# Letting the V side of a cross-covariance attention kernel fall behind and close after the loop

## The chip, the cores and the metric

The kernel runs on one core of one Trainium2 chip. The metric is the device time of a launch in microseconds (us), as the median of several executions. The profiles are taken in single executions; their span, from the first to the last instruction, is 1.7 to 1.8 us shorter than the device time of the same execution (two executions of one experiment differ by 2.1 and 3.0 us). Each run is filed as fast or slow; here slow means over 1.5% above the fastest run of the same kernel.

In lines of the profile PE is TensorE (PEld its weight loads), DVE is VectorE, ACT is ScalarE, POOL is GpSimd, and SPq is the queue of SyncE, which issues the transfers. The strips cut the span into 40 slices: PEclk is the clock granted to TensorE and DMA the busy share of the transfer engines, both in tenths. In a timeline the name after the line number is the operation, then written tile `<-` read tiles; `vb`, `vps`, `vt`, `po` and `so` are a V unit after the cast, its transposes, their copy, its product and the evicted product.

## The reference

```python
batch, heads, seq, dim = 8, 12, 512, 64                       # Q, K, V: float32
Q_norm = Q / (norm(Q, axis=-2) + 1e-10); K_norm = K / (norm(K, axis=-2) + 1e-10)
attn = softmax(einsum('bhnd,bhne->bhde', Q_norm, K_norm))     # 64 x 64 for each head
out  = einsum('bhnd,bhde->bhne', V, attn)
```

There are 96 heads. The kernel takes four at a time, a "unit", so 24 units. For each unit Q, K, V and the output are one transfer of 512 KB each.

## The kernel before

The two sides of a unit use different data until the last product. The attention side casts Q and K to bf16, forms Gram matrices, norms, logits and exponentials, normalises the result and writes a second copy of it ("doubled"). The V side casts V, transposes it on TensorE, evicts the transposes (copies them out of PSUM, the memory in which this kernel places what TensorE writes), multiplies by the attention matrix and evicts the product in two halves.

```python
def cast_v(u, copy=nc.scalar.copy):
    w = vb[u] = vbp.tile([128, SV, TP, 2 * D], BF16, name="vb")          # 3 buffers
    copy(w.rearrange("p s t d -> p s (t d)"), vf[u])

def vtrans(u):
    ps = ps_v.tile([128, SV, TP, 128], BF16, name="vps")                 # 1 buffer in PSUM
    for g in range(SV):
        for t in range(TP):
            nc.tensor.transpose(ps[:, g, t, :], vb[u][:, g, t, :], identb)
    w = vt[u] = vtp.tile([128, SV, TP, 128], BF16, name="vt")            # 3 buffers
    nc.scalar.copy(w, ps)

def outs(u):
    ...                                          # 2 halves of 8 matmuls into PSUM (po, 2 buffers)
        nc.scalar.copy(s[:, g], po)              # one eviction for each half

for s in range(U):                               # one iteration carries pieces of several units
    on(load_qk, s + 3); on(load_v, s + 1); on(store, s - 6)
    on(cast_v, s - 1);  on(cast_q, s + 1)
    on(scale_k, s - 1); on(normalise, s - 2)
    on(grams, s);       on(norms, s);    on(cast_k, s + 1)
    on(doubled, s - 2); on(keep_kq, s)
    on(outs, s - 3)
    on(logits, s - 1);  on(scale_q, s - 1); on(exps, s - 1)
    on(vtrans, s - 1)
...                                              # the last attention steps and outs(21), outs(22), outs(23)
```

The schedule is manual: the program's order is the order of each engine's instructions. In the trace of the kernel before, TensorE, VectorE and ScalarE start theirs in that order throughout iteration 23 and the tail; on VectorE, for instance, the normalisation of unit 22 starts at 123.17 us, the V cast after it at 123.51 and the first step of the next normalisation at 124.11. All 96 transfers are issued from SyncE, in one order.

Of the kernel before, what the change touches and what calls it, by code (L numbers as in the profile page):

```python
# [24 lines left out]
def kernel(  # L25
# [7 lines left out]
    nc = tc.nc  # L33
    B, H, N, _ = Q.shape
    assert N == NV * R and Q.shape[3] == D
    U = B * H // HU
# [17 lines left out]
    ps_o = ctx.enter_context(tc.tile_pool(name="ps_o", bufs=2, space=bass.MemoryType.PSUM))  # L54

    LOAD_AHEAD = 3
    V_AHEAD = LOAD_AHEAD - 2
    STORE_LAG = 6

    qf, kf, vf, vb, qkb, nsq, rq, kqs, sl, ex, vt, so, kq = ({} for _ in range(13))  # L60

    def load_qk(u):
        qf[u] = qp.tile([128, R, D], F32, name="qf")
        kf[u] = qp.tile([128, R, D], F32, name="kf")
        nc.sync.dma_start(out=qf[u].rearrange("p t d -> p (t d)"), in_=Qf[u])  # L65
        nc.sync.dma_start(out=kf[u].rearrange("p t d -> p (t d)"), in_=Kf[u])  # L66

    def load_v(u):
        vf[u] = vp.tile([128, SV, TP * 2 * D], F32, name="vf")
        nc.sync.dma_start(out=vf[u], in_=Vf[u])  # L70

    def store(u):
        nc.sync.dma_start(out=Of[u], in_=so[u].rearrange("p s t d -> p s (t d)"))
# [8 lines left out]
    def cast_v(u, copy=nc.scalar.copy):  # L82
        w = vb[u] = vbp.tile([128, SV, TP, 2 * D], BF16, name="vb")
        copy(w.rearrange("p s t d -> p s (t d)"), vf[u])  # L84
# [25 lines left out]
    def scale_k(u):  # L110

        kk = kqs[u] = small.tile([128, HU, D], F32, name="kqs")
        nc.vector.tensor_tensor(  # L113
            out=kk[D:], in0=kq[u][D:], in1=rq[u][D:, :, None].to_broadcast([D, HU, D]), op=ALU.mult,
        )

    def logits(u):
        for h in range(HU):
            nc.tensor.transpose(lg[:, h, :], kqs[u][D:, h, :], ident[D:, D:])  # L119
# [9 lines left out]
    def normalise(u):  # L129
        s = small.tile([D, HU], F32, name="esum")  # L130
        nc.vector.reduce_sum(out=s, in_=ex[u], axis=AX.X)
        ri = small.tile([D, HU], F32, name="rinv")
        nc.vector.reciprocal(ri, s)
        a = abuf[u % len(abuf)]
        nc.vector.tensor_tensor(out=a[0:D, :, 0, :], in0=ex[u], in1=ri[:, :, None].to_broadcast([D, HU, D]), op=ALU.mult)  # L135

    def vtrans(u):

        ps = ps_v.tile([128, SV, TP, 128], BF16, name="vps")
# [3 lines that stand above are left out]
        w = vt[u] = vtp.tile([128, SV, TP, 128], BF16, name="vt")  # L143
        nc.scalar.copy(w, ps)  # L144

    def doubled(u):

        a = abuf[u % len(abuf)]
        nc.tensor.matmul(dup[D:], identb[0:D, 0:D], a[0:D, :, 0, :], tile_position=(0, D))  # L149
        nc.scalar.copy(a[D:, :, 1, :], dup[D:])  # L150

    def outs(u):
        s = so[u] = sop.tile([128, SV, TP, 2 * D], F32, name="so")
        a = abuf[u % len(abuf)]
        for g in range(SV):
            po = ps_o.tile([128, TP, 2 * D], F32, name="po")
            for t in range(TP):
                for x in range(2):
                    rows = slice(MV * x, MV * (x + 1))
                    nc.tensor.matmul(  # L160
                        po[rows, t, :], vt[u][:, g, t, rows],
                        a[:, 2 * g + x].rearrange("p a d -> p (a d)"), tile_position=(0, MV * x),
                    )
            nc.scalar.copy(s[:, g], po)  # L164

    gbuf = ps_g.tile([128, HU, 512], F32, name="gram")
    ltile = ps_l.tile([128, 2, HU, D], F32, name="lgdup")
# [3 lines left out]

    for u in range(LOAD_AHEAD):
        load_qk(u)
        if u - 2 >= 0:
            load_v(u - 2)

    ident = const.tile([128, 128], F32, name="ident")
    make_identity(nc, ident)
# [2 lines left out]
    mhalf = const.tile([128, HU], F32, name="mhalf")  # L181
    nc.gpsimd.memset(mhalf, -0.5)
    abuf = []
    for i in range(3):
        a = const.tile([128, HU, 2, D], BF16, name=f"ab{i}")
        nc.gpsimd.memset(a, 0.0)
        abuf.append(a)

    def on(f, u):
        if 0 <= u < U:  # L190
            f(u)

    on(cast_q, 0)
    on(cast_k, 0)
    for s in range(U):
        on(load_qk, s + LOAD_AHEAD)
        on(load_v, s + V_AHEAD)
        on(store, s - STORE_LAG)
        on(cast_v, s - 1)
        on(cast_q, s + 1)  # L200
        on(scale_k, s - 1)
        on(normalise, s - 2)
        on(grams, s)
        on(norms, s)
        on(cast_k, s + 1)
        on(doubled, s - 2)
        on(keep_kq, s)
        on(outs, s - 3)
        on(logits, s - 1)
        on(scale_q, s - 1)  # L210
        on(exps, s - 1)
        on(vtrans, s - 1)


    last = U - 1
    scale_k(last)
    logits(last)
    scale_q(last)
    exps(last)
    normalise(last - 1)  # L220
    doubled(last - 1)
    outs(last - 2)
    cast_v(last, nc.vector.tensor_copy)
    normalise(last)
    doubled(last)
    vtrans(last)
    outs(last - 1)
    outs(last)
    for u in range(U - STORE_LAG, U):
        store(u)  # L230


# [28 lines left out]
```

## Time and profile before

| | before |
|---|---|
| device time, median of 3 runs | 134.80 us (134.79 to 135.32) |
| span of the profiled run | 134.2 us |
| bytes moved | 50.34 MB in 96 transfers |
| busy share PE / DVE / ACT / POOL | 67 / 71 / 72 / 28 % |

No engine is busy three quarters of the time, and the strip of the DMA engines reads 9 nearly everywhere. The prediction shows those lines. The busy shares average over a long middle, where transfers set the pace (DMA is 79% of the chain of waits), and a tail of 14 us, where a chain of small dependent steps does. A transfer lands 10.1 to 10.3 us after its issue (medians), and one takes 1.28 us at 409 GB/s; by estimate from these two about eight are under way at once. The change is about the tail.

### The profile page before, as it was taken

How to read it: one execution, taken by the hardware profiler on the slowest of the kernel's cores; microseconds unless marked ns; L12 is line 12 of the kernel's file. 1: busy time of each engine (PE TensorE's matmuls, PEld its weight loads, DVE VectorE, ACT ScalarE, POOL GpSimd, SP SyncE). 2: the span in 40 equal slices, each digit the busy share in tenths (PEclk: the TensorE clock that was granted, in tenths of full speed). 3: DMA queues.
4: the chain of work that ended last, by engine and by line, in shares of the span. 5: the costliest groups of instructions: out<-in, count | busy, mean ns of one | idle time of the engine just before them, and what ended most of it. 6: DMA issues, size and time to landing. Idle time of an engine off the chain costs nothing.

```text
span 134.2 us, 5393 instructions
## 1 busy us (share of the span) xinstructions
PE 89.5 (67%) x2232; PEld 69.9 (52%) x2232; DVE 95.6 (71%) x361; ACT 96.5 (72%) x168; POOL 37.3 (28%) x35
## 2 busy tenths in 40 slices
PE   0137659786689997864866766776776399964930
PEld 0136538664468685643744644555555287652720
DVE  0447859999998698989669679679679397767300
ACT  3000857989999789896867966966965779797760
POOL 7004440543225325431230330330330303311000
PEclk9999999999955558999689689779779755798555
DMA  4999999999999999999999999999999999998454
GB/s 150 330 393 412 401 402 404 398 396 404 398 401 407 411 402 415 403 405 408 405 411 417 400 412 410 413 407 419 401 413 401 416 407 400 406 385 316 153 201 173
DMA packets 19992, 50.67 MB, mean 378 GB/s; under 512 B 1537, under 2 KB 1537, under 8 KB 19969
## 3 DMA queue, kind: packets, MB, share of 16 engines
q1 hardware_dynamic: 19968, 50.34, 96.4%
q8 instruction: 17, 0.28, 0.8%
q14 instruction: 7, 0.05, 0.1%
HBM read 37.75 MB, written 12.58 MB: 375 GB/s over the span
## 4 chain that ended last, share of the span: by engine, by line
DMA 79%; ACT 7%; SPq 3%; PE 3%; issue 2%; DVE 2%; DVEq 0%; ACTq 0%
DMA vf<-in_V_dram 71%; DMA qf<-in_Q_dram 8%; ACT vb L84 2%; ACT so L164 2%; SPq L66 2%; SPq L65 1%; PE lgdup L119 1%; PE po L160 1%; ACT ab L150 1%; PE vps L142 1%; ACT vt L144 1%; DVE sl L123 1%; PE lgdup L149 1%; SPq L70 0%; DVE kqs L113 0%
## 5 line engine op out<-in xcount | busy, mean ns | idle before, releaser
L108 POOL TENSOR_TENSOR rq<-nsq,mhalf 128x4 f32<-128x4 f32 x24 | 34.9, 1453 | 83.2 <-DVE nsq L103 83.2
L91 PE MATMUL gram<-qkb 32*128 32x128 bf16 x1536 | 36.9, 264 | 9.3 <-DVE qkb L80 8.7
L91 PEld LDWEIGHTS <-qkb 32*128 32x128 bf16 x1536 | 31.1, 118 | 13.3 <-DVE qkb L80 9.0
L84 ACT CAST vb<-vf 128x1024 bf16<-128x1024 f32 x23 | 24.1, 1047 | 17.4 <-DMA vf<-in_V_dram 17.4
L164 ACT COPY so<-po 128x512 f32<-128x512 f32 x48 | 25.8, 589 | 0.9 <-PE po L160 0.2
L160 PEld LDWEIGHTS <-vt 128*64 128x64 bf16 x384 | 15.0, 133 | 19.3 <-issue 18.8
L144 ACT COPY vt<-vps 128x1024 bf16<-128x1024 bf16 x24 | 24.0, 1000 | 1.2 <-PE vps L142 0.9
L103 DVE CUSTOM_DVE_ANT_0 scr<-gram,ident 128x128 f32<-128x128 f32 x96 | 22.0, 282 | 2.3 <-PE gram L91 2.0
L77 DVE CAST qkb<-qf 128x1024 bf16<-128x1024 f32 x24 | 16.5, 686 | 7.9 <-DMA qf<-in_Q_dram 7.6
L123 DVE TENSOR_TENSOR sl<-lgdup,rq 64x256 f32<-64x256 f32 x24 | 10.0, 416 | 15.2 <-PE lgdup L119 13.7
L142 PE MATMUL vps<-identb,vb 128*128 128x128 bf16 x192 | 19.2, 260 | 1.7 <-ACT vb L84 1.7
L160 PE MATMUL po<-ab,vt 128*64 128x128 bf16 x384 | 19.5, 259 | 0.6 <-ACT so L164 0.6
L119 PE MATMUL lgdup<-ident,kqs 64*64 64x64 f32 x96 | 11.4, 249 | 12.7 <-ACT ab L150 12.1
L149 PE MATMUL lgdup<-ab,identb 64*64 64x256 bf16 x24 | 8.0, 334 | 15.6 <-DVE ab L135 15.2
L80 DVE CAST qkb<-kf 128x1024 bf16<-128x1024 f32 x24 | 16.4, 685 | 0.5 <-DMA kf<-in_K_dram 0.5
L142 PEld LDWEIGHTS <-vb 128*128 128x128 bf16 x192 | 14.1, 116 | 4.6 <-ACT vb L84 1.9
L119 PEld LDWEIGHTS lgdup<-ident,kqs 64*64 64x64 f32 x96 | 7.0, 122 | 16.6 <-ACT ab L150 14.9
L96 ACT COPY kq<-gram 64x256 f32<-64x256 f32 x24 | 8.8, 367 | 9.1 <-DVE nsq L103 8.8
L150 ACT CAST ab<-lgdup 64x256 bf16<-64x256 f32 x24 | 8.8, 367 | 3.1 <-PE lgdup L149 2.7
L113 DVE TENSOR_TENSOR kqs<-kq,rq 64x256 f32<-64x256 f32 x24 | 10.1, 422 | 1.1
L127 ACT ACTIVATE ex<-sl 64x256 f32<-64x256 f32 x24 | 10.0, 418 | 1.0 <-DVE sl L123 1.0
L135 DVE TENSOR_TENSOR ab<-ex,rinv 64x256 bf16<-64x256 f32 x24 | 10.0, 417 | 0.8
(15 smaller groups left out, 28.9 us busy)
## 6 DMA issues: line engine op xcount, KB each, us to landing
qf<-in_Q_dram SPq DMA_DIRECT2D x24, 512.0 KB, 10.3
kf<-in_K_dram SPq DMA_DIRECT2D x24, 512.0 KB, 10.3
vf<-in_V_dram SPq DMA_DIRECT2D x24, 512.0 KB, 10.3
out_dram<-so SPq DMA_DIRECT2D x24, 512.0 KB, 10.1
```

Of the source, the lines that this page charges most:

```text
L77: nc.vector.tensor_copy(qkb[u][:, :, 0:D], qf[u])
L80: nc.vector.tensor_copy(qkb[u][:, :, D:], kf[u])
L84: copy(w.rearrange("p s t d -> p s (t d)"), vf[u])
L91: nc.tensor.matmul(gbuf[:, h, 0:2 * D], x, x, start=(t == 0), stop=(t == R - 1), tile_position=(NV * h, 0))
L103: nc.vector.tensor_tensor_reduce(out=scr, in0=gbuf[:, h, 0:2 * D], in1=ident, scale=1.0, scalar=1e-20, op0=ALU.mult, op1=ALU.add, accum_ou ...
L108: nc.gpsimd.tensor_tensor(out=r, in0=n2, in1=mhalf, op=ALU.pow)
L119: nc.tensor.transpose(lg[:, h, :], kqs[u][D:, h, :], ident[D:, D:])
L123: nc.vector.tensor_tensor(out=s, in0=lg, in1=rq[u][0:D, :, None].to_broadcast([D, HU, D]), op=ALU.mult)
L142: nc.tensor.transpose(ps[:, g, t, :], vb[u][:, g, t, :], identb)
L144: nc.scalar.copy(w, ps)
L160: nc.tensor.matmul(po[rows, t, :], vt[u][:, g, t, rows], a[:, 2 * g + x].rearrange("p a d -> p (a d)"), tile_position=(0, MV * x),)
L164: nc.scalar.copy(s[:, g], po)
```

## The change

The intent, in the words that came with it: the V side runs at 19/22 of the rate of the attention side and falls back up to 5 units; the rest of it closes the program. Q and K then arrive earlier, and the end of the program still has V loads and stores to keep the DMA engines busy. The diff, cut to its core:

```diff
+    def outs_by(s):
+        return max(0, (s - 2) * 19 // 22)
-    def outs(u):
+    def outs(u, copies=(nc.scalar.copy, nc.scalar.copy)):
-            nc.scalar.copy(s[:, g], po)
+            copies[g](s[:, g], po)
-    for i in range(3):                          # buffers of the attention matrix
+    for i in range(9):
     for s in range(U):
+        n0, n1 = outs_by(s - 1), outs_by(s)
-        on(load_v, s + V_AHEAD)
-        on(store, s - STORE_LAG)
-        on(cast_v, s - 1)
+        ...                                     # V loads up to n1 + 2, stores up to n1 - 4, casts up to n1
-        on(outs, s - 3)
+        for v in range(n0, n1):
+            outs(v)
-        on(vtrans, s - 1)
+        ...                                     # the transposes of the units cast in this iteration
     ...                                         # after the loop: the last attention steps, outs(18)
-    cast_v(last, nc.vector.tensor_copy)
-    vtrans(last)
-    outs(last - 1)
-    outs(last)
+    both = (nc.scalar.copy, nc.vector.tensor_copy)
+    for u in range(n1 + 1, U):                  # 19 to 23
+        cast_v(u, nc.vector.tensor_copy)
+        vtrans(u)
+        outs(u, both)
+        store(u)
```

More of the change, by code (lines that the diff above doesn't have):

```diff
@@ L56 @@
     LOAD_AHEAD = 3
-    V_AHEAD = LOAD_AHEAD - 2
-    STORE_LAG = 6
+    def outs_by(s):
+        return max(0, (s - 2) * 19 // 22)
     qf, kf, vf, vb, qkb, nsq, rq, kqs, sl, ex, vt, so, kq = ({} for _ in range(13))
@@ L173 @@
         load_qk(u)
-        if u - 2 >= 0:
-            load_v(u - 2)
     ident = const.tile([128, 128], F32, name="ident")
@@ L194 @@
     on(cast_k, 0)
+    on(load_v, 0)
+    on(load_v, 1)
+    nv, nst, nt = 2, 0, 0
     for s in range(U):
+        n0, n1 = outs_by(s - 1), outs_by(s)
         on(load_qk, s + LOAD_AHEAD)
-        on(load_v, s + V_AHEAD)
-        on(store, s - STORE_LAG)
-        on(cast_v, s - 1)
+        while nv < min(U, n1 + 3):
+            load_v(nv)
+            nv += 1
+        while nst < n1 - 3:
+            store(nst)
+            nst += 1
+        new = range(nt, n1 + 1) if s >= 1 else ()
+        for v in new:
+            cast_v(v)
         on(cast_q, s + 1)
@@ L211 @@
         on(exps, s - 1)
-        on(vtrans, s - 1)
+        for v in new:
+            vtrans(v)
+            nt = v + 1
+    for u in range(nv, U):
+        load_v(u)
+    for u in range(nst, U):
+        if u >= n1:
+            break
+        store(u)
+        nst += 1
     last = U - 1
+    both = (nc.scalar.copy, nc.vector.tensor_copy)
     scale_k(last)
@@ L221 @@
     doubled(last - 1)
-    outs(last - 2)
-    cast_v(last, nc.vector.tensor_copy)
+    outs(n1)
+    store(n1)
     normalise(last)
     doubled(last)
-    vtrans(last)
-    outs(last - 1)
-    outs(last)
-    for u in range(U - STORE_LAG, U):
+    for u in range(n1 + 1, U):
+        cast_v(u, nc.vector.tensor_copy)
+        vtrans(u)
+        outs(u, both)
         store(u)
```

## The prediction

> **What bounds the kernel now.** I began with the page's slices, because two strips tell apart a kernel limited by transfers from one limited by an engine.
>
> ```profile
> PEclk9999999999955558999689689779779755798555
> DMA  4999999999999999999999999999999999998454
> GB/s 150 330 393 412 401 402 404 398 396 404 398 401 407 411 402 415 403 405 408 405 411 417 400 412 410 413 407 419 401 413 401 416 407 400 406 385 316 153 201 173
> ```
>
> One slice is 134.2/40 = 3.36 us. From the third slice to the thirty-sixth, which is about 7 to 120.9 us, the 16 DMA engines are full at some 405 GB/s; only the last four slices sag. Each of Q, K, V and the output moves in 24 transfers of 512 KB, 96 in all and 50.34 MB. At 409 GB/s (the stretch 60 to 100 us) one takes 0.5243/409 = 1.28 us, and 96 take 123 us. Everything above that is start-up and tail.
>
> The chain that ended last agrees:
>
> ```profile
> DMA 79%; ACT 7%; SPq 3%; PE 3%; issue 2%; DVE 2%; DVEq 0%; ACTq 0%
> ```
>
> So I looked at the tail in stages (columns: stretch, length, busy time and count for PE, PE weight loads, DVE, ACT, POOL, then granted clock, DMA share, GB/s):
>
> ```profile
> 118.00:120.00 2.00, 1.19 (x45) 0.76 (x33) 1.84 (x11) 1.98 (x4) 0.00 (x0) 1.00 1.04 402
> 120.00:122.00 2.00, 1.22 (x16) 0.95 (x16) 0.84 (x2) 1.98 (x6) 1.01 (x1) 1.00 0.76 295
> 122.00:124.00 2.00, 0.51 (x6) 0.16 (x5) 1.74 (x5) 1.13 (x2) 0.00 (x0) 0.70 0.92 344
> 124.00:126.00 2.00, 1.78 (x23) 1.31 (x23) 1.11 (x4) 1.72 (x4) 0.00 (x0) 0.50 0.29 113
> 126.00:128.00 2.00, 1.61 (x22) 1.30 (x21) 0.00 (x0) 1.43 (x3) 0.00 (x0) 0.50 0.69 260
> 128.00:130.00 2.00, 1.13 (x16) 0.84 (x15) 0.00 (x0) 1.72 (x4) 0.00 (x0) 0.50 0.23 86
> ```
>
> From 120 us to the end the DMA engines move 3.1 MB in 14.2 us, where 7.6 us would do. About 6.6 us are lost, of which the last store's own latency must stay. The change can win at most some 4 to 5 us. Two things to keep: the tail runs at half clock, and its work is a chain of small dependent pieces. The timeline of the tail, engine by engine:
>
> ```profile
> 123.17 0.42 DVE L135 TENSOR_TENSOR ab<-ex,rinv 64x256 bf16<-64x256 f32 x1
> 123.51 0.68 DVE L84 CAST vb<-vf 128x1024 bf16<-128x1024 f32 x1
> ...
> 125.58 1.03 PE L142 MATMUL vps<-identb,vb 128*128 128x128 bf16 x8
> ...
> 126.66 1.01 ACT L144 COPY vt<-vps 128x1024 bf16<-128x1024 bf16 x1 [0.57 <-PE vps L142]
> ...
> 128.21 1.13 PE L160 MATMUL po<-ab,vt 128*64 128x128 bf16 x16 [0.59 <-ACT so L164]
> ...
> 128.88 1.07 ACT L164 COPY so<-po 128x512 f32<-128x512 f32 x2 [0.24 <-PE po L160]
> ```
>
> Read it as one unit's V path: cast, 8 transposes, one eviction, 16 matmuls, two evictions. Each engine executes in the order of the program (the cast of the last V stands on VectorE exactly between the two normalisations, as the source has it).
>
> [...] 0.50 from 124 us on, where PE works in bursts; the 8 transposes take 1.03 us there and 0.62 us at full clock. [...] DVE's 64x256 fp32 operation out of PSUM takes 0.416 us and its 128x128 one 0.282, so 128 elements cost 0.134 us and the fixed part is 0.148. [...]
>
> **The change part by part.** No bytes and no arithmetic are removed.
>
> (1) The attention side runs ahead. Counting transfers in issue order, before has K of the last unit as number 83 and the V that iteration 22 waits for (unit 21) as number 84. After, outs_by(23) = 21*19//22 = 18, so the loop has done 18 outputs and not 21. Its last K is number 76, and the V for iteration 22 (now unit 17) is number 77. That is 7 transfers earlier, at 1.28 us: 9.0 us. V 18, which gates iteration 23, follows two transfers later, as before. Before, that V's cast in iteration 22 began at 114.90 on landing and the cast of iteration 23 at 118.80; after, I put the latter at T = 109.8 us. Is the compute fast enough? An iteration now carries 2 + 2*19/22 = 3.73 transfers, 4.78 us. ACT's work before is 96.5/24 = 4.02 us per unit and DVE's 95.6/24 = 3.98; measured iterations took 4.1 us at full clock around 30 us and about 4.5 at half clock. So the loop stays bound by transfers, narrowly.
>
> (2) Six fresh 128x512 memsets on POOL, 6*0.5 = 3 us. POOL finished its own at 3.1 us and first works again at 10.1. Hidden.
>
> (3) The drained loop. Before, from 118.80, the normalisation of unit 22 ended at 123.60 (T+4.8) and that of 23 at 125.18 with a V cast of 0.6 between them. After, unit 23's ends near T+5.8. The outputs of 18 occupy PE to T+6.2; then the last doubling; transposes of 19 end near T+7.55, their eviction T+8.6, its outputs T+9.7, its DVE eviction T+10.4 = 120.2 us.
>
> (4) The closing loop, units 19 to 23: cast, transposes, outputs and store for one unit, then the next. Its cast and its second eviction are both on DVE. DVE being in order, the cast of 20 can't start until the eviction of 19's second half is done, which needs the outputs, which need the transposes, which need the cast of 19. The five units therefore do not overlap at all. One period at half clock: cast 0.68 + hop 0.04 + transposes until the eviction starts 1.08 (125.58 to 126.66) + eviction 1.01 + hop 0.05 + 16 matmuls 1.09 + DVE eviction 128x512 (estimate from the fit above: 0.148 + 512*0.134/128 = 0.68) = 4.63 us. At full clock transposes take 0.67 and matmuls 0.68, and the period is 3.8 us. ACT's half of the eviction (0.59) ends inside DVE's.
>
> (5) The end. Unit 19 is done at 120.2; four more periods, 18.5 us: 138.7. Before, the last store was issued at 129.97 and the span ended 4.2 us later; so the span becomes 142.9. Timed runs are 0.6 us above the profiled span (134.8 to 134.2): 143.5 us. At full clock throughout: 4*3.8 = 15.2 and about 0.8 saved in unit 19, 138.7 + 0.6 = 139.3 us.
>
> And the transfers? Number 90 (the store of 17) lands near 122.4 as the DMA engines stay full up to there. After it only six stores remain, 7.7 us of transfer, but the compute hands over one every 4.6 us. The gap at the end that the change wanted to fill grows: a store of 1.28 us per 4.63 us is a DMA share of about 0.28.
>
> **The rivals.** *The intent holds:* outputs of the deferred units run under the queue of loads and stores and the end is at the DMA floor: 123 us + some 2.7 at the start + the last latency 3 gives about 129.5 us, -4%. For it: after the loop six units instead of three are left, whose loads, outputs and stores could overlap. Against it: it needs one unit per 1.3 to 2.1 us, which ACT (1.01 + 0.59) and PE (2.1 at half clock) could do if units overlapped, and the order on DVE forbids that. *It evens out:* if some unit overlap that I do not see brings the period to 2.4 us, the 9.0 us won at the loop's end are just paid back and the time stays at 135. *The clock recovers:* 139.3, as above. PE would be busy 2.1 of 4.63 us in bursts; before, a stretch at 116 to 118 us recovered after PE had been nearly continuously busy from 110 us, while the sparse tail stayed at 0.50. I give recovery a chance of 3 in 10. *The loop turns compute-bound:* if half clock lasts through most of the loop, 24 iterations of about 4.6 us put T one or two us later, 144 to 146 us.
>
> **How the range follows.** Half clock 143.5 at 7 in 10 and full clock 139.3 at 3 in 10 average 142.2; a late loop pulls up a little. I predict 142.6 us, range 139.0 to 145.5. Faster by over 2%: 0.06 [...]; within 2%: 0.06; slower: 0.88.
>
> **What would show it.** The last 20 us should be five equal pieces of 4 to 4.7 us, each cast, transposes, eviction, matmuls, eviction; the chain that ended last should lose most of its DMA share after about 116 us to DVE, PE and ACT in alternation; the strip of DMA should read full to about 122 us, then 2 or 3 tenths. DVE casts of vb should be 5 and DVE evictions into so 5, at about 0.68 us. The last gram should start near 108 us and not 117. I am wrong if the cast of unit 20 starts before the eviction of 19, or if DMA stays full past 126 us; in size, if the period leaves 3.8 to 4.7 us.

Unit 19 done at 120.2 us, four periods of 4.63, 4.2 to the end of the span and 0.6 to the device time come to 143.5 us at half clock and, at full clock, to 139.3; 7 to 3 that is 142.2, and with a little for a late loop 142.6. The 0.50 and the times of the transposes that stand between two cuts are the granted clock and its effect in the trace before. The 0.68 of the eviction on VectorE is the estimate from two other operations of that trace. The argument about VectorE rests on the order seen there (123.17, 123.51, 124.11). In the first rival the 2.7 and the 3 are estimates, too: the first 6 us move 231 GB/s, which is 2.6 us short of 409, and from the last store's issue to the end of the span are 4.2 us, of which its transfer takes 1.28.

## The result, and the profile after

| | before | after |
|---|---|---|
| device time, median of 4 runs | 135.06 us (134.79 to 135.78) | 143.88 us (143.21 to 144.99) |
| ratio | | 1.0652 (95% interval 1.0565 to 1.074) |
| span of the profiled run | 134.2 us | 142.6 us |

The changed kernel is 6.5% slower. Here and below a ratio is the mean time of one kernel's fast runs over that of the other's of the same rounds, so it is not quite the ratio of the medians.

The slices of the profile after, one being 142.6/40 = 3.57 us:

```profile
PEclk9999999999999999857975799658995955555555
DMA  4999999999999999999999999999999998533033
GB/s 176 315 406 406 398 409 410 398 399 402 401 405 403 417 401 415 395 407 413 407 416 405 407 414 408 411 407 408 405 403 404 398 402 336 221 150 142 29 123 147
```

The DMA engines are as full as before up to about 121 us, but then they run at about half or less for six slices and not for three. The chain of waits of the profile after:

```profile
DVE 32%; PE 22%; POOL 17%; DMA 11%; issue 8%; ACT 4%; SPq 2%; POOLq 1%; ACTq 0%; DVEq 0%
```

DMA had 79% of this chain before and has 11% now. The end of the program is no longer reached through transfers. The timeline of one closing unit (number 20), and the first step of the next, shows what reaches it; the columns are start, duration, engine, line, operation, and in brackets the idle time before it with what ended it.

```profile
120.22 0.68 DVE L87 CAST vb<-vf 128x1024 bf16<-128x1024 f32 x1
...
120.96 1.03 PE L145 MATMUL vps<-identb,vb 128*128 128x128 bf16 x8 [1.39 <-DVE vb L87]
122.08 1.01 ACT L147 COPY vt<-vps 128x1024 bf16<-128x1024 bf16 x1 [2.31 <-PE vps L145]
...
123.14 1.06 PE L163 MATMUL po<-ab,vt 128*64 128x128 bf16 x16 [1.16 <-ACT vt L147]
123.83 0.59 ACT L167 COPY so<-po 128x512 f32<-128x512 f32 x1 [0.73 <-PE po L163]
124.25 0.69 DVE L167 COPY so<-po 128x512 f32<-128x512 f32 x1 [3.35 <-PE po L163]
124.86 0.68 DVE L87 CAST vb<-vf 128x1024 bf16<-128x1024 f32 x1
```

Each step up to the eviction on VectorE starts within a tenth of a us after the one before it has ended, on another engine, which has idled since its own last step. (ScalarE's half of the eviction, at 123.83, starts while the second half of the matmuls still runs.) The next cast has no idle time in front of it: it has been standing in VectorE's order behind the eviction at 124.25 and starts 0.61 us after that one's start, 0.08 before its recorded end. (So have the other three that follow an eviction, each 0.61 us after its start.) The casts start at 115.52, 120.22, 124.86, 129.51 and 134.16. From the second on the spacing is 4.64 to 4.65 us; apart from that 0.08 us nothing overlaps from one unit to the next.

The stages of the closing loop (stretch, length, busy time and count of PE, PE weight loads, DVE, ACT, POOL, then granted clock, DMA share, GB/s) show no engine busy for much more than half of the time, and the clock at half:

```profile
122.00:126.00 4.00, 1.46 (x20) 1.23 (x21) 1.29 (x2) 1.60 (x2) 0.00 (x0) 0.50 0.35 129
126.00:130.00 4.00, 1.70 (x22) 1.19 (x20) 1.10 (x2) 1.60 (x2) 0.00 (x0) 0.50 0.32 122
130.00:134.00 4.00, 2.10 (x24) 1.59 (x24) 0.64 (x2) 1.60 (x2) 0.00 (x0) 0.50 0.35 131
```

The account of the two spans closes. Take the start of iteration 23's V cast on ScalarE: 118.80 before, 109.12 after, so the lag did bring the loop's end forward, by 9.7 us. From there to the end of the last eviction it took 11.15 us before (129.95) and 29.76 after (138.88). The sum is +18.6 - 9.7 = +8.9 us at the last eviction. The rest, up to the end of the span, was 4.2 us before and 3.7 after.

### The profile page after: what moved, and what is told of

Same layout as the page of the kernel before. It is cut to its first block, busy times and chain, and to the rows that moved or that the text cites. A ratio compares the mean times of both kernels' runs of the same rounds, so it can differ in the third digit from the quotient of the medians.

```text
span 142.6 us, 5388 instructions
## 1 busy us (share of the span) xinstructions
PE 89.9 (63%) x2232; PEld 70.0 (49%) x2232; DVE 101.3 (71%) x370; ACT 91.2 (64%) x159; POOL 42.3 (30%) x41
## 4 chain that ended last, share of the span: by engine, by line
DVE 32%; PE 22%; POOL 17%; DMA 11%; issue 8%; ACT 4%; SPq 2%; POOLq 1%; ACTq 0%; DVEq 0%
POOL rq L111 17%; DVE scr L106 9%; DMA qf<-in_Q_dram 9%; PE po L163 7%; PE vps L145 6%; PE gram L94 6%; DVE kqs L116 5%; DVE ab L138 5%; DVE esum L134 5%; ACT vt L147 3%; DMA out_dram<-so 2%; DVE rinv L136 2%; PE lgdup L122 2%; DVE vb L87 2%; PE lgdup L152 2%
## 5 line engine op out<-in xcount | busy, mean ns | idle before, releaser
L111 POOL TENSOR_TENSOR rq<-nsq,mhalf 128x4 f32<-128x4 f32 x24 | 37.1, 1548 | 69.3 <-DVE nsq L106 69.3
L167 ACT COPY so<-po 128x512 f32<-128x512 f32 x43 | 23.3, 589 | 4.3 <-PE po L163 3.9
L80 DVE CAST qkb<-qf 128x1024 bf16<-128x1024 f32 x24 | 18.0, 749 | 7.1 <-DMA qf<-in_Q_dram 7.1
L87 ACT CAST vb<-vf 128x1024 bf16<-128x1024 f32 x19 | 19.9, 1046 | 2.9 <-DMA vf<-in_V_dram 2.9
L167 DVE COPY so<-po 128x512 f32<-128x512 f32 x5 | 3.5, 691 | 16.8 <-PE po L163 16.8
```

The lines of the kernel that those rows point to most:

```text
L80: nc.vector.tensor_copy(qkb[u][:, :, 0:D], qf[u])
L111: nc.gpsimd.tensor_tensor(out=r, in0=n2, in1=mhalf, op=ALU.pow)
L167: copies[g](s[:, g], po)
```

## The experiments

All kernels below gave correct results. Each was run beside the kernel before on the same chip. The experiments ran on three chips, on which the median of the kernel before was 134.79, 135.49 and 135.61 us; a difference between two experiments from different chips is that much less certain than its ratio to before.

### The next cast ahead of the evictions

My theory was that VectorE's order makes the five units serial. One line is moved; the instructions are the same and as many.

```diff
+    cast_v(n1 + 1, nc.vector.tensor_copy)
     for u in range(n1 + 1, U):
-        cast_v(u, nc.vector.tensor_copy)
         vtrans(u)
+        if u + 1 < U:
+            cast_v(u + 1, nc.vector.tensor_copy)
         outs(u, both)
```

> The closing loop of the changed kernel with one line moved: the V cast of the next unit is placed on VectorE ahead of this unit's evictions, not after them. Same instructions, same count. My theory (VectorE executes in order, so the cast of unit u+1 waits for the eviction of u, and the five units run one after another with a period of 4.64 us): the ring through VectorE is opened and what is left is a ring through PE alone, transposes 1.12 + eviction 1.06 + matmuls 1.05 = 3.2 us at half clock; four periods of 1.4 us less, 143.9 - 5.7 = 138.2 us, or nearer 135 if the denser PE work brings the full clock back (period 2.4). Rival (the tail is set by something else, the stores' own latency or the number of transfers): no change, 143.9.

Measured: 138.19 us (137.52 to 139.55), ratio to before 1.0238 (1.0136 to 1.0341). The timeline of this run:

```profile
120.70 1.06 PE L163 MATMUL po<-ab,vt 128*64 128x128 bf16 x16 [1.16 <-ACT vt L147]
121.38 0.59 ACT L167 COPY so<-po 128x512 f32<-128x512 f32 x1 [0.73 <-PE po L163]
121.70 1.03 PE L145 MATMUL vps<-identb,vb 128*128 128x128 bf16 x8
121.81 0.69 DVE L167 COPY so<-po 128x512 f32<-128x512 f32 x1 [1.90 <-PE po L163]
122.42 0.68 DVE L87 CAST vb<-vf 128x1024 bf16<-128x1024 f32 x1
122.83 1.01 ACT L147 COPY vt<-vps 128x1024 bf16<-128x1024 bf16 x1 [0.85 <-PE vps L145]
123.89 1.06 PE L163 MATMUL po<-ab,vt 128*64 128x128 bf16 x16 [1.16 <-ACT vt L147]
```

The transposes at 121.70 now start right behind the matmuls, before the eviction on VectorE has begun. The period is 123.89 - 120.70 = 3.19 us, as expected. The rival, that the tail is set by the stores, would have left the time at 143.9 and falls.

### Both evictions on ScalarE

This undoes another part of the change and gives ScalarE more work.

```diff
-    both = (nc.scalar.copy, nc.vector.tensor_copy)
+    both = (nc.scalar.copy, nc.scalar.copy)
```

> The changed kernel with both evictions of a closing unit on ScalarE, as in the kernel before; the split over ScalarE and VectorE is undone. ScalarE then carries 1.01 + 0.59 + 0.59 per unit, VectorE only the casts, which can run ahead. My theory: the ring through VectorE is opened just as in the run with the cast moved, so the period is again 3.2 us and the time 138.2, although an engine gets more work. Rival (the closing loop is bound by the work of its engines, and the split is what makes it bearable): 0.59 us more per unit, 143.9 + 5*0.59 = 146.9.

Measured: 138.05 us (137.25 to 138.82), ratio 1.0194 (1.0109 to 1.0279). The time is that of the run with the cast moved, although 0.59 us per unit went to the busier engine, and so is the period: the matmuls start at 118.88, 122.06 and 125.25. The closing loop was therefore bound by order and not by the work of an engine: with the casts on VectorE, putting an eviction there too is what tied the knot.

### No lag

```diff
-        return max(0, (s - 2) * 19 // 22)
+        return max(0, (s - 2) * 22 // 22)
```

> The changed kernel at rate 22/22 in place of 19/22: the V side keeps pace, the loop ends with 21 outputs done and the closing loop, still unit after unit, has 2 units and not 5. My theory: each unit fewer to close saves one period of 4.64 us and costs two transfers (a V load and a store) that now come before the last K, 2.57 us: net 2.07 us per unit, so 143.9 - 6.2 = 137.7 us, still 2% above before because two units are closed one after another instead of overlapping. Rival (the number of units left does not matter, the tail is a fixed cost): within 1 us of 143.9. Rival (lag gives nothing, all of 4.64 comes back): 130.

Measured: 137.23 us (136.86 to 137.31), ratio 1.0128 (1.0059 to 1.0198). Three units fewer to close gave 6.7 us, against an expected 6.2. One net number does not show two terms, but the trace of this run does. Its closing period is 4.64 us again (the two evictions on VectorE start at 126.41 and 131.05), and the V cast of iteration 23 starts at 116.47 in place of 109.12: 7.35 us later for three units, 2.45 each, where 2.57 was expected for two transfers.

### Nine buffers alone

The kernel before with the six extra memsets, so one part of the change by itself.

```diff
-    for i in range(3):
+    for i in range(9):
```

> The kernel before with one part of the change alone: nine buffers for the attention matrix, so six more memsets on GpSimd at the start. In the changed kernel's trace the first cast on VectorE took 2.37 us and not 0.69 and ended with the last memset, and the first Gram started 0.94 us later. My theory: the transfers are full anyway from the third slice on and the first iterations have slack, so nothing of it reaches the end: within 0.5% of before, with the long first cast in the trace. Rival: the start is on the path, and 0.9 us of the change's 8.8 come from it: 0.7% slower.

Measured: 135.35 us (134.48 to 136.54; the last is slow and outside the ratio), ratio 0.9975 (0.9919 to 1.003): the same. The start of its timeline shows the cost that does not reach the end:

```profile
1.64 4.22 POOL L186 MEMSET ab<- 128x512 bf16 x9
3.94 2.46 DVE L77 CAST qkb<-qf 128x1024 bf16<-128x1024 f32 x1 [3.94 <-DMA qf<-in_Q_dram]
```

The first cast takes 2.46 us in place of 0.69 and ends 0.54 us after the memsets do, as far as POOL's recorded spans, which are rough, can tell.

### The half clock

Throw-away matmuls keep PE busy in the closing loop, into a PSUM buffer that nobody reads any more.

```diff
         vtrans(u)
+        warm(14)                                # 128x128 matmuls of the identity
         outs(u, both)
+        warm(20)
```

> The changed kernel with idle work for PE in the closing loop: 14 throw-away 128x128 matmuls after each unit's transposes and 20 after its matmuls, into the Gram's PSUM buffer that nobody reads any more. Result unchanged. It tests the term of the period that I sized by the half clock. If the clock follows PE's activity, it returns to 1.0 a few us into the loop and the period falls from 4.64 to 3.8 us: four times 0.83 less, 140.6 us (139.5 to 142 with the first unit still slow), with a granted clock near 1 in the last 15 us. If the clock stays at 0.5 the throw-away matmuls stand in the way: 34 at some 0.11 us, of which about 2.4 us fit into PE's waits, 1.2 us more per unit, about 149 us.

Measured: 140.13, 141.09 and 141.50 us in the fast runs, ratio 1.0406 (1.0346 to 1.0467). The fourth run, the profiled one, took 178.38 us and was slow.

> The same kernel as the run with throw-away matmuls, whose profile fell in a slow execution of 178 us while its three timed runs took 140.1 to 141.5; this look is for a profile of a fast one. Theory: closing units of about 3.8 us each with the granted clock at 1.0, time 140 to 142 us. If the fast runs have periods near 4.6 us, the clock term of my sum is not what they gained by.

Measured: one run, 142.03 us, its state unknown by itself. The device time exceeds its span by 3.0 us, where 1.7 to 1.8 us is usual; the span, 139.0 us, lies among those of the fast runs (138.4 to 139.4). The stages of its closing loop:

```profile
116.00:120.00 4.00, 4.00 (x51) 3.63 (x50) 0.64 (x2) 2.17 (x4) 0.00 (x0) 0.58 0.98 379
120.00:124.00 4.00, 3.50 (x66) 3.07 (x64) 1.48 (x4) 1.60 (x2) 0.00 (x0) 1.00 0.61 230
124.00:128.00 4.00, 3.46 (x65) 3.00 (x62) 1.48 (x3) 1.60 (x2) 0.00 (x0) 1.00 0.36 136
```

The granted clock returns to 1.00 by 120 us and stays there; by the modelled ends PE is then busy for 3.26 to 3.50 of each 4 us, against 1.46 to 2.10 at a clock of 0.50 in the changed kernel. What share of busy time goes with which clock is not shown: from 110 to 116 us the kernel before kept PE busy for 5.71 of 6 us at 0.50 to 0.51, and in the last units of the fastest version below 1.19 of 2 us went with 1.00. The casts then start at 119.97, 123.78, 127.58 and 131.39, a period of 3.80 to 3.81 us. The clock term of my period is confirmed at both clocks: 4.64 at half, 3.81 at full. Adding work to a loop that was bound by waits made it faster (1.0406 against 1.0652, each to the kernel before).

### Cast and transposes one unit ahead

```diff
+    cast_v(n1 + 1, nc.vector.tensor_copy)
+    vtrans(n1 + 1)
     for u in range(n1 + 1, U):
-        cast_v(u, nc.vector.tensor_copy)
-        vtrans(u)
+        if u + 1 < U:
+            cast_v(u + 1, nc.vector.tensor_copy)
+            vtrans(u + 1)
         outs(u, both)
```

> The cast and the transposes of the next closing unit both stand ahead of this unit's outputs, so that units overlap on PE too. My theory: the period falls to PE's own work, 1.03 + 1.06 = 2.1 us at half clock, or to ScalarE's 1.01 + 0.59 = 1.6 us if the clock comes back; four periods of 2.5 us less, 143.9 - 10.2 = 133.7 us (132 to 135), about the time before. The lag is then worth nothing much: below the time before by at most 2%. Rival 1 (the lag itself costs, through the loop): stays above 138. Rival 2 (the lag's idea was right and only its closing was written badly): below 132.

Measured: 137.97 us (137.53 to 138.13), ratio 1.0183 (1.0112 to 1.0255). This expectation missed by 4.3 us. The time alone would nearly fit its first rival, that the lag itself costs in the loop ("above 138"); the trace and the next run speak against it. The timeline of the run says why:

```profile
123.00 0.69 DVE L167 COPY so<-po 128x512 f32<-128x512 f32 x1 [2.13 <-PE po L163]
123.61 0.68 DVE L87 CAST vb<-vf 128x1024 bf16<-128x1024 f32 x1
124.35 1.03 PE L145 MATMUL vps<-identb,vb 128*128 128x128 bf16 x8 [1.39 <-DVE vb L87]
125.31 1.06 PE L163 MATMUL po<-ab,vt 128*64 128x128 bf16 x16
...
126.42 0.69 DVE L167 COPY so<-po 128x512 f32<-128x512 f32 x1 [2.13 <-PE po L163]
```

The ring through VectorE is still closed, one unit further on. The cast at 123.61 belongs to the unit after next and stands behind the eviction at 123.00; PE meets its transposes (124.35) before the matmuls of the next unit (125.31), whose input was ready at 123.06; and their eviction closes the ring. The period is 126.42 - 123.00 = 3.42 us. I had counted the engines' work and overlooked that two engines which keep the program's order, here VectorE and PE, make a ring across units.

### Casts two units ahead

```diff
+    cast_v(n1 + 1, nc.vector.tensor_copy)
+    cast_v(n1 + 2, nc.vector.tensor_copy)
+    vtrans(n1 + 1)
     for u in range(n1 + 1, U):
-        cast_v(u, nc.vector.tensor_copy)
-        vtrans(u)
+        if u + 2 < U:
+            cast_v(u + 2, nc.vector.tensor_copy)
+        if u + 1 < U:
+            vtrans(u + 1)
         outs(u, both)
```

> The run with cast and transposes of the next unit ahead came out at 138.0 and not 133.7. Its trace shows a ring that I had overlooked: the cast two units on still stands behind this unit's eviction on VectorE, and PE, in order, runs the transposes that wait for it ahead of the next unit's matmuls: 0.61 + 0.73 + 0.97 + 1.1 = 3.42 us. Here the casts run two units ahead. If that ring was the cause, the period falls to transposes + their eviction in one PSUM buffer, 1.12 + 1.06 = 2.2 us: the last eviction comes some 3.8 us earlier, 134.2 us (133.3 to 135). Rival (something else holds the period, as PSUM or the clock): 138 again.

Measured: 133.66 us (132.67 to 134.60), ratio 0.988 (0.9813 to 0.9946), against an expected 134.2. Three lines of its timeline (those between them are left out):

```profile
120.18 0.69 DVE L167 COPY so<-po 128x512 f32<-128x512 f32 x1 [3.15 <-PE po L163]
120.30 1.01 PE L145 MATMUL vps<-identb,vb 128*128 128x128 bf16 x8 [0.16 <-ACT vt L147]
122.35 0.69 DVE L167 COPY so<-po 128x512 f32<-128x512 f32 x1 [0.88 <-PE po L163]
```

The ring was the cause. The period is 122.35 - 120.18 = 2.17 us while the transposes still take 1.01, near the 1.03 that they took at a clock of 0.50 in the changed kernel; they now wait for the eviction of the transposes before them and no longer for a cast. From 122.47 on the transposes take 0.61: the clock came back (0.95 from 122 to 124 us, 1.00 from there to 128), and the remaining periods are 1.42 to 1.68. So a part of the gain, not separated here, is the clock's, which the expectation had not counted. With the same lag, the same transfers and the same instructions, the changed kernel is now 10.2 us faster and 1.2% faster than before.

### The closing begun among the last attention steps

As above, and the first closing unit's cast and transposes, and the second one's cast, go where VectorE and PE wait anyway.

```diff
     scale_k(last)
+    cast_v(n1 + 1, nc.vector.tensor_copy)
     logits(last)
     scale_q(last)
     exps(last)
+    vtrans(n1 + 1)
     normalise(last - 1)
+    cast_v(n1 + 2, nc.vector.tensor_copy)
     doubled(last - 1)
```

> As the run with casts two ahead, and the first closing unit's cast and transposes (and the next one's cast) are put among the last attention steps, where VectorE and PE wait anyway. The closing units then start about one period of 2.2 us earlier, the last eviction ends near 126.5 us, and the stores, one per 1.28 us from number 90 at 122.4 us on, become the bound: 132.8 us (131.8 to 133.8), 1.5 to 2% below before. Rival (the closing is bound by what the last attention unit hands over): no gain over two ahead, 134.2.

Measured: 132.85 us (132.04 to 133.30; 6 runs), ratio 0.9808 (0.9766 to 0.985), as expected (132.8). This is the fastest version and beats both kernels; whether by 2% over the kernel before is unclear. Its interval overlaps that of the version above, so the gain of the early start alone is not settled. Its slices and a stage of its tail (131.5/40 = 3.29 us a slice):

```profile
DMA  4899999999999999999999999999999999999893
```

```profile
124.00:126.00 2.00, 1.19 (x32) 0.95 (x28) 0.69 (x1) 1.78 (x3) 0.00 (x0) 1.00 0.90 346
126.00:128.00 2.00, 0.00 (x0) 0.00 (x0) 0.69 (x1) 0.31 (x1) 0.00 (x0) 0.78 0.90 338
```

The DMA engines stay at about 0.9 up to 128 us and PE's clock is back at 1.00 in the last units. Little is left to fill, so the transfers are nearer to being the bound again, as the change intended: they make up 30% of this run's chain of waits, against 11% in the changed kernel and 79% in the kernel before.

### The same closing without lag

```diff
-        return max(0, (s - 2) * 19 // 22)
+        return max(0, (s - 2) * 22 // 22)
```

> The early, overlapped closing of the fastest version at rate 22/22, without lag: two units to close instead of five. It asks whether the lag itself is worth anything or the better closing does it all. My theory: the loop ends some 7.5 us later (6 transfers of 1.28 us more before the last K), the last eviction comes about 10.5 us after iteration 23 begins plus one period of 2.2, near 130.5 us, and the time is 135 to 136 us, as before; the lag, once its closing is overlapped, is worth 2.5 us. Rival (the lag is worthless, the overlap is all): 132.9, as with the lag.

Measured: 133.78 us (133.62 to 134.67), ratio 0.9923 (0.987 to 0.9976). The direction was right and the size was not: the lag is worth about 1.15% (0.9923 - 0.9808), some 1.5 us, and I had expected 2.5. Iteration 23 began at 117.46, half a us after the estimate (109.45 in the run with lag, plus 7.5), but the last eviction ended at 129.20, where I had put it near 130.5: the last unit has no transposes in front of its matmuls, so it cost 1.84 us after the one before it, and the first came sooner, too. So better overlap alone takes back the serial closing's loss (137.23 to 133.78), and the lag adds its 1.5 us only on top of it. The two ratios come from different chips, each against the kernel before on its own. Nor is the 1.5 us shown to be the lag's alone: without lag the granted clock stayed at 0.50 from 122 us to the end, while with it the last units ran at 1.00.

## Why the prediction was right, point by point

The predicted time was 142.6 us (range 139.0 to 145.5); measured 143.88. The 142.6 is a mean of two cases weighted by their chances, and neither of them; the case that came true, half clock, was put at 143.5.

1. *The loop ends earlier, near T = 109.8.* Measured 109.12. The step stands, though the transfer that V 17's cast waits for landed 9.7 us earlier than its counterpart before (105.22 against 114.90) where I had counted 9.0; the runs do not show why. V 17's cast still waited 0.52 us for its transfer, while the cast after it did not wait, so the "narrowly" was apt: at the loop's end compute and transfers are nearly even, and the chain of waits in the loop now runs through POOL and DVE.
2. *The memsets are hidden.* They are (ratio 0.9975 alone), though not for the reason I gave. I looked only at POOL's own idle time; VectorE's first cast, which starts while the memsets run, took 2.37 us in the changed kernel and 2.46 with nine buffers alone, against 0.69 with three, where it starts 1.05 us after they have ended. Why is not shown. That the slack of the transfer-bound loop hides the delay is my reading; no run tests it apart.
3. *The first closing unit is done at 120.2.* Measured 119.61 + 0.69 = 120.30. Here luck helped, as two small errors cancel: T came 0.7 earlier, and the last attention unit's steps 0.7 later relative to T, its Gram taking 1.89 us at a granted clock of 0.50, and 1.07 at 1.00 in the kernel before.
4. *The five units do not overlap, period 4.63.* Measured 4.64. The cause is shown by two separate edits that open VectorE's order (138.19 and 138.05 us) and by the dose (6.7 us for three units). The estimated DVE eviction of 0.68 was measured at 0.69, but it counts 0.61 in the ring, since the next cast starts before its recorded end; the four other steps take 4.03 and not 3.95, so here, too, small errors cancel. The fit behind the 0.68 was an estimate from two operations of different kinds, and they do not show that reading PSUM sets their time: the 64x256 operation that reads none (line 135) takes as long, 0.417 us. Measured in the closing loop, the eviction of 512 elements out of PSUM takes 0.69 us, and the cast of 1024 out of SBUF 0.68.
5. *Half clock at 7 in 10.* The profiled run had 0.50 throughout the closing loop, and the run with throw-away matmuls, at 1.00, gave 3.81 in place of the 3.80 predicted.
6. *The end.* The span was put at 142.9 and was 142.6. The step from span to device time was wrong: I took the median of the timed runs less one profiled span, 0.6 us. In nearly every run that lists both they differ by 1.7 to 1.8 us (two executions of one experiment differ by 2.1 and 3.0 us); the profiled execution of the kernel before was itself one of the longer of its kind, at 135.93 us. The error is small beside the range.
7. *The gap grows.* It did, and by the predicted size. The stages above read 0.32 to 0.35 and not 0.28 mainly because stretches of 4 us do not hold whole periods; the two periods from 124.94 to 129.59 and from there to 134.24 have a DMA share of 0.30 each, at 114 and 113 GB/s.

One rival was put too low. I gave the intent 129.5 us if units overlapped. They can be made to overlap, and the best version that does so measured 132.85. The three terms that I named add up to 128.7, so the 129.5 holds at most 0.8 of the 1.75 us of device time beyond the span; the rest of the gap is time in the tail in which the transfers are not full (a share of 0.9 at best after 120 us).

## What to carry to other kernels

Count the period of a drained loop along the dependencies and each engine's order in the program, not along the engines' work: here, with the program naming unit after unit, a unit's first and last instruction on the same engine left no overlap but 0.08 us (4.64 us a unit, and 3.19 once either was moved), and prefetching by one unit left the same ring one unit further on (3.42). Deferring work to the end paid here only once the deferred work was pipelined; unpipelined, each unit cost 4.64 us and gave back about 2.5. In a tail where PE works in bursts, size PE's terms at the clock that the trace shows there (here 0.50).
